# Gate and up products of a feature tile in two PSUM chains, with T4 negated: an fp32 hybrid encoder on one Trainium2 core

## The chip, the cores and the metric

The kernel runs on one core of a Trainium2 chip. The metric is device time in microseconds (us) of one execution. The engines are TensorE (PE: matmuls, and PEld: its weight loads), VectorE (DVE), ScalarE (ACT), GpSimd (POOL) and SyncE (SP, which issues most DMAs). Each engine takes its instructions in the order in which the program has them; engines wait for one another by semaphores. Results of matmuls land in PSUM, in banks of 128 x 512 fp32 values; VectorE and ScalarE read them from there.

## The reference

Two batches (512 prompt and 256 sample tokens, 768 in all, width 1024) go through two layers of an encoder. A layer is a mixer (differential attention beside a bidirectional mLSTM) and a gated feed-forward part with a convolution over positions. The change touches only this part:

```python
def _conv_ffn(x, w_gu, conv_w, conv_b, w_down):
    gu = x @ w_gu
    gate, up = gu[..., :D_FF], gu[..., D_FF:]          # D_FF = 2816
    gp = jnp.pad(gate, ((0, 0), (half, half), (0, 0)))
    conv = conv_b.astype(gate.dtype) + sum(gp[:, j:j + S] * conv_w[j] for j in range(CONV_WIDTH))
    hmid = jax.nn.gelu(conv, approximate=False) * up
    return hmid.astype(x.dtype) @ w_down
```

All is fp32.

## The kernel before

A matrix product in fp32 is made of three matmuls on parts: each operand is split into a high and a low part (hi and lo), and hi hi, hi lo, lo hi are added up in PSUM. The split of a weight block of 128 x 512 is a "conversion": ScalarE writes the high part wh (line 171), VectorE subtracts it for the low part wl (line 172). Weights come by DMA on SP's queue into a ring of six pieces (raw), and their parts go into twelve slots; a slot is filled again when the product that used it has ended.

The feed-forward part takes the 2816 features as 22 tiles of 128 per layer. For a tile it needs gate and up, each 128 features x 768 tokens. It computes both as one 2 x 2 block product by the scheme of Strassen and Winograd: seven products in place of eight. The tokens' blocks are A11, A12, A22 and the sums S1 to S4, all made once per layer. The weights' blocks are g0, g1, u0, u1 (halves of the rows of gate and up) and the combinations T1 to T4, which POOL (T1, T3) and VectorE (T2, T4) make at line 149 for each tile. A product is 12 matmuls of 128x384 at line 915 (four steps over k, three passes) into one bank. `bank()` hands out banks in turn by the string FTAGS of six tags; there are three banks of tag d, two of s, one of t, u and L each.

A tile's function `ff_tile` writes its seven products p1, p2, p4, p6, p7, p5, p3 one after the other, and the sums of Winograd's scheme between them: ScalarE copies p1 (line 927, m1), VectorE does the rest in seven operations with one operand in PSUM (lines 931 to 947). Then follow the convolution over positions (ScalarE line 948, VectorE lines 950 and 951, each in two pieces), the gelu (line 952), the product with up (line 953) and its split into high and low parts (lines 957, 958). g_lo, g_hi, up_lo, up_hi in this document are the halves of gate and up by tokens.

Tiles come in groups of 3 (the last of 4). After the first tile of the next group `down(gi)` multiplies the group's results by w_down (matmuls of 128x512, line 975) and VectorE adds the products to `acc` (line 982; for the first group line 980). The banks for this are of tags t and u in turn, and the three of d in the last group, after which the second LayerNorm follows tile by tile.

A scheduler sets the order on each engine: it takes instructions as they are ready, by a priority that is their place in the program, less an offset (for conversions of weights 100 places earlier). So the products of one tile and the next can be interleaved on TensorE.

## Time and profile before

| | us |
|---|---|
| median of 3 runs | 1888.2 (1887.25 to 1888.33) |
| the profiled execution: span from first to last instruction | 1882.1 |
| TensorE busy | 1838.9 (98%) |
| VectorE busy | 1342.5 (71%) |
| ScalarE busy | 771.7 (41%) |
| GpSimd busy | 238.8 (13%) |

The span is the time from the first to the last instruction that the profiler recorded; what lies around it belongs to the device time too. Matmuls overlap in the array, so that the listed duration of one (some 340 ns) is longer than the distance from one to the next, and that distance is what counts. In rows of a timeline the columns are start in us, duration in us, engine, line, operation, output and inputs, and in brackets the idle time of the engine before it with what ended it; "x2" means two instructions in a row.

### The profile page before, as it was taken

Reading aid. Unit: us, or ns where it says so; the run is one execution under the profiler, and the core shown is the slowest. Engines: PE = TensorE matmul, PEld = TensorE weight load, DVE = VectorE, ACT = ScalarE, POOL = GpSimd, SP = SyncE. Lnnn points to the kernel's source line nnn. Section 1 sums busy time; section 2 is a strip of 40 time slices with the busy share of each in tenths; the row PEclk is TensorE's granted clock in tenths of the full one; section 3 lists DMA queues with packets and bytes.
Section 4 is the critical chain, followed back from the end, with each engine's and each line's share of the span. In section 5 each row is a group of like instructions: output and inputs, shape, how many; then the busy total and the mean of one; then the engine's idle time right before and its main releaser. Section 6 shows DMA issues by size and latency. Waiting matters only on the chain. (4 is left out here: it accounts for less than half of the span.)

```text
span 1882.1 us, 26221 instructions
## 1 busy us (share of the span) xinstructions
PE 1838.9 (98%) x9692; PEld 1592.7 (85%) x9692; DVE 1342.5 (71%) x2576; ACT 771.7 (41%) x1624; POOL 238.8 (13%) x256
## 2 busy tenths in 40 slices
PE   8899999999999999999998999999999999999998
PEld 8777777779899899899897777777898998998996
DVE  5445776489886786787954457765898877877878
ACT  4344565334443343343332445654253432433330
POOL 1000101042110111110110011010411111111102
PEclk9999999999999999999999999999999999999999
DMA  6212110311222121122233021104022221221221
GB/s 196 85 49 68 46 45 23 135 40 62 85 81 66 59 82 62 64 77 87 100 107 90 18 68 51 40 23 150 25 68 96 68 79 62 71 76 57 79 62 67
DMA packets 83279, 134.94 MB, mean 72 GB/s; under 512 B 7984, under 2 KB 27056, under 8 KB 83152
## 3 DMA queue, kind: packets, MB, share of 16 engines
q1 hardware_dynamic: 82432, 132.90, 22.0%
q8 instruction: 76, 1.25, 0.3%
q14 instruction: 51, 0.42, 0.1%
q10 hardware_dynamic: 720, 0.37, 0.1%
HBM read 126.86 MB, written 6.39 MB: 71 GB/s over the span
## 5 line engine op out<-in xcount | busy, mean ns | idle before, releaser
L915 PE MATMUL p<-actA,wh 128*128 128x384 f32 x1408 | 363.4, 338 | 3.2 <-DVE g L940 3.2
L171 ACT ACTIVATE wh<-raw 128x512 fp32r<-128x512 f32 (+1 forms) x348 | 215.7, 629 | 299.8 <-PE p L915 109.7
L172 DVE TENSOR_TENSOR wl<-raw,wh 128x512 fp32r<-128x512 f32 (+1 forms) x348 | 242.7, 707 | 95.9 <-ACT wh L171 95.4
L915 PE MATMUL p<-actB,wh 128*128 128x384 f32 x1056 | 270.1, 337 | 0.0
L915 PEld LDWEIGHTS p<-actA,wh 128*128 128x128 f32 x1408 | 254.7, 188 | 5.8 <-DVE g L940 3.8
L915 PE MATMUL p<-actA,wl 128*128 128x384 f32 x704 | 237.3, 337 | 0.0
L149 POOL TENSOR_TENSOR T<-raw,raw 128x512 f32<-128x512 f32 x88 | 120.7, 1374 | 836.5 <-DVE wl L172 483.6
L975 PE MATMUL dn<-wh,actB 128*128 128x512 f32 x576 | 208.7, 396 | 1.1 <-DVE acc L982 1.1
L171 ACT ACTIVATE wh<-T 128x512 fp32r<-128x512 f32 x176 | 108.3, 628 | 220.2 <-DVE acc L982 105.0
L915 PEld LDWEIGHTS p<-actB,wh 128*128 128x128 f32 x1056 | 191.2, 188 | 0.0
L975 PE MATMUL dn<-wh,ring 128*128 128x512 f32 x480 | 179.2, 397 | 1.8 <-DVE acc L982 1.8
L915 PE MATMUL p<-actB,wl 128*128 128x384 f32 x528 | 177.2, 336 | 0.0
L982 DVE TENSOR_TENSOR acc<-acc,dn 128x512 f32<-128x512 f32 x144 | 98.1, 681 | 72.0 <-PE dn L975 71.8
L172 DVE TENSOR_TENSOR wl<-T,wh 128x512 fp32r<-128x512 f32 x176 | 129.6, 748 | 22.1 <-ACT wh L171 21.9
L975 PEld LDWEIGHTS dn<-wh,actB 128*128 128x128 f32 x576 | 108.0, 188 | 28.7 <-DVE acc L982 2.8
L915 PEld LDWEIGHTS p<-actA,wl 128*128 128x128 f32 x704 | 132.2, 188 | 0.1
L871 PE MATMUL wo<-wh,actB 128*128 128x512 f32 x384 | 122.7, 396 | 0.0
L975 PE MATMUL dn<-wl,actB 128*128 128x512 f32 x288 | 113.2, 393 | 0.0
L975 PEld LDWEIGHTS dn<-wh,ring 128*128 128x128 f32 x480 | 90.0, 188 | 24.8 <-DVE acc L982 4.4
L915 PEld LDWEIGHTS p<-actB,wl 128*128 128x128 f32 x528 | 99.1, 188 | 0.0
L356 PE MATMUL aqkA<-actA,wh 128*128 128x512 f32 x256 | 97.7, 407 | 0.0
L975 PE MATMUL dn<-wl,ring 128*128 128x512 f32 x240 | 94.6, 394 | 0.0
(263 smaller groups left out, 3442.8 us busy)
## 6 DMA issues: line engine op xcount, KB each, us to landing
raw<-in_w_g_dram SPq DMA_DIRECT2D x88, 256.0 KB, 2.7
raw<-in_w_u_dram SPq DMA_DIRECT2D x88, 256.0 KB, 2.7
raw<-in_w_down_dram SPq DMA_DIRECT2D x88, 256.0 KB, 2.9
raw<-in_w_out_dram SPq DMA_DIRECT2D x32, 256.0 KB, 2.6
pt<-scr_m SPq DMA_DIRECT2D x12, 512.0 KB, 5.9
raw<-in_w_c_dram SPq DMA_DIRECT2D x16, 264.0 KB, 3.9
raw<-in_w_av_dram SPq DMA_DIRECT2D x16, 256.0 KB, 4.8
raw<-in_w_aq_dram SPq DMA_DIRECT2D x16, 256.0 KB, 3.5
```

The source lines that it names most:

```text
L149: src["engine"].tensor_tensor(out=src["tile"], in0=a, in1=b, op=ALU.subtract)
L171: self.nc.scalar.activation(h, v, AF.Identity)
L172: self.nc.vector.tensor_tensor(out=l, in0=v, in1=h.bitcast(F32), op=ALU.subtract)
L356: PE.matmul(psA, w, actA[:, k, b, SB:T], start=n == 0, stop=n == 23)
L871: PE.matmul(p, actB[:, k, a, t * 128:(t + 1) * 128], units[k][1 + b], start=n + i == 0, stop=n == 7 and i == 2)
L915: PE.matmul(ps, blk[1 + a][:, k * 128:(k + 1) * 128], x[:, k, b, :], start=k + i == 0, stop=k == 3 and i == 2)
L975: PE.matmul(p, x, (wh_, wl_)[b], start=k + i == 0, stop=k == nf - 1 and i == 2)
L982: V.tensor_tensor(out=z, in0=z, in1=p, op=ALU.add)
```

## The change

- Three turns of `bank()` per tile in place of seven. A11, S2, S3 and A22 go into one bank px without its being cleared between, S1 and S4 into a second, pz; A12 has p2. Between the products of px its partial sum is copied to SBUF by ScalarE: m1 after A11, u2 after S2, u3 after S3, and g_hi at the end. pz is read after S1 (up_hi = pz + u3) and after S4 (up_lo = pz + u2).
- The order of a tile's products is A11, A12, S2, S1, S3, S4, A22.
- T4 has the other sign (g1 - T2), so that A22's product can be added into px. The order of the weight blocks follows the products.
- The sums on VectorE are three for a tile (g_lo, up_hi, up_lo), the copies on ScalarE four.

The rest of the diff takes out comments.

```diff
-                t4 = {"a": t2, "b": g1, "tag": "T4", "engine": V}
-                for src in (t4, t2, t3, t1, u1) if i in early else (g0, g1, t4, t2, t3, t1, u1):
+                t4 = {"a": g1, "b": t2, "tag": "T4", "engine": V}
+                for src in (t2, t1, t3, u1, t4) if i in early else (g0, g1, t2, t1, t3, u1, t4):
                     W.block(src, 512)
...
-        def product(ps, x):
+        def product(ps, x, first=True, last=True):
             blk = W.take()
             for k in range(4):
                 for i, (a, b) in enumerate(PASSES):
-                    PE.matmul(ps, blk[1 + a][:, k * 128:(k + 1) * 128], x[:, k, b, :], start=k + i == 0, stop=k == 3 and i == 2)
+                    PE.matmul(ps, blk[1 + a][:, k * 128:(k + 1) * 128], x[:, k, b, :], start=first and k + i == 0,
+                              stop=last and k == 3 and i == 2, skip_group_check=True)
             W.done(blk)
...
-            p1 = bank(f"p1_{f}")
-            product(p1, A11)
-            S.copy(m1, p1)
+            px = bank(f"px_{f}")
+            product(px, A11, last=False)
+            S.copy(m1, px)
             p2 = bank(f"p2_{f}")
             product(p2, A12)
             yield
             V.tensor_tensor(out=g[:, lo_], in0=p2, in1=m1, op=ALU.add)
-            p4 = bank(f"p4_{f}")
-            product(p4, A22)
-            p6 = bank(f"p6_{f}")
-            product(p6, S2)
-            V.tensor_tensor(out=u2, in0=p6, in1=m1, op=ALU.add)
-            p7 = bank(f"p7_{f}")
-            product(p7, S3)
-            V.tensor_tensor(out=u3, in0=p7, in1=u2, op=ALU.add)
-            V.scalar_tensor_tensor(out=g[:, hi_], in0=p4, scalar=-1.0, in1=u3, op0=ALU.mult, op1=ALU.add)
-            p5 = bank(f"p5_{f}")
-            product(p5, S1)
-            V.tensor_tensor(out=u4, in0=p5, in1=u2, op=ALU.add)
-            V.tensor_tensor(out=up[:, hi_], in0=p5, in1=u3, op=ALU.add)
-            p3 = bank(f"p3_{f}")
-            product(p3, S4)
-            V.tensor_tensor(out=up[:, lo_], in0=p3, in1=u4, op=ALU.add)
+            product(px, S2, first=False, last=False)
+            S.copy(u2, px)
+            pz = bank(f"pz_{f}")
+            product(pz, S1, last=False)
+            product(px, S3, first=False, last=False)
+            S.copy(u3, px)
+            V.tensor_tensor(out=up[:, hi_], in0=pz, in1=u3, op=ALU.add)
+            product(pz, S4, first=False)
+            product(px, A22, first=False)
+            S.copy(g[:, hi_], px)
+            V.tensor_tensor(out=up[:, lo_], in0=pz, in1=u2, op=ALU.add)
```

Three places in the first layer's tile 8, an ordinary one, show what this does to the order. In the names the number behind the first underscore is the tile; p6, p7 and p4 are the products with S2, S3 and A22; numbers behind wh and wl count the weight blocks, and the last number is the buffer's. "waits" lists the semaphores (an engine, or a DMA queue of the hardware) that the instruction waits for.

TensorE before, from the end of A22's product through S2's to the start of S3's:

```order
L915 MATMUL p4_8_5758<-actA_70,wl147_5532 128x384
L915 MATMUL p6_8_5777<-actB_2870,wh148_5537 128x384 x2
L915 MATMUL p6_8_5777<-actB_2870,wl148_5538 128x384
L915 MATMUL p6_8_5777<-actB_2870,wh148_5537 128x384 x2
L915 MATMUL p6_8_5777<-actB_2870,wl148_5538 128x384
L915 MATMUL p6_8_5777<-actB_2870,wh148_5537 128x384 x2
L915 MATMUL p6_8_5777<-actB_2870,wl148_5538 128x384
L915 MATMUL p6_8_5777<-actB_2870,wh148_5537 128x384 x2
L915 MATMUL p6_8_5777<-actB_2870,wl148_5538 128x384
L915 MATMUL p7_8_5797<-actB_2870,wh149_5543 128x384 [waits DVE_49]
```

TensorE after, from S3's product to the start of S4's:

```order
L915 MATMUL px_8_5667<-actB_2870,wh149_5499 128x384 x2
L915 MATMUL px_8_5667<-actB_2870,wl149_5500 128x384
L915 MATMUL px_9_5822<-actA_70,wh152_5566 128x384 x2
L915 MATMUL px_9_5822<-actA_70,wl152_5567 128x384
L915 MATMUL px_9_5822<-actA_70,wh152_5566 128x384 x2
L915 MATMUL px_9_5822<-actA_70,wl152_5567 128x384
L915 MATMUL px_8_5667<-actA_70,wh151_5547 128x384 [waits Activation_49]
L915 MATMUL px_8_5667<-actA_70,wh151_5547 128x384
L915 MATMUL px_8_5667<-actA_70,wl151_5548 128x384
L915 MATMUL px_8_5667<-actA_70,wh151_5547 128x384 x2
L915 MATMUL pz_8_5728<-actA_70,wh150_5525 128x384 [waits DVE_49]
L915 MATMUL pz_8_5728<-actA_70,wh150_5525 128x384
```

Before, a product runs through its twelve matmuls, and waits only for the reader that a bank had some products earlier. After, S3's product is followed by six matmuls of the next tile (px_9), then five of A22 into px_8, which wait for ScalarE, then S4 into pz_8, which waits for VectorE.

ScalarE before, from the split of tile 7 to the conversion that follows tile 8's convolution:

```order
L957 ACTIVATE ring_4085<-up7_5551 128x384 [waits DVE_49]
L957 ACTIVATE ring_4085<-up7_5551 128x384
L171 ACTIVATE wh158_5749<-raw127_5535 128x512 [waits DMAHW1_49,PE_49]
L171 ACTIVATE wh159_5771<-raw129_5592 128x512 [waits DMAHW3_49,PE_49]
L171 ACTIVATE wh160_5790<-raw130_5594 128x512 [waits DMAHW4_49,PE_49]
L171 ACTIVATE wh161_5810<-raw131_5655 128x512 [waits DMAHW5_49,PE_49]
L948 ACTIVATE c8_5713<-g8_5711,convw_220 128x768 [waits DVE_49,Activation_49]
L171 ACTIVATE wh162_5831<-raw132_5697 128x512 [waits DMAHW6_49,PE_49]
```

ScalarE after, from the copy u2 to the copy u3 and the conversion behind it:

```order
L935 COPY u2_8_5665<-px_8_5667 128x384 [waits PE_49]
L954 ACTIVATE ring_4075<-up7_5507 128x384 [waits DVE_49]
L954 ACTIVATE ring_4075<-up7_5507 128x384
L171 ACTIVATE wh160_5741<-raw130_5551 128x512 [waits DMAHW4_49,PE_49]
L171 ACTIVATE wh161_5759<-raw131_5608 128x512 [waits DMAHW5_49,PE_49]
L939 COPY u3_8_5666<-px_8_5667 128x384 [waits PE_49]
L171 ACTIVATE wh162_5779<-raw132_5646 128x512 [waits DMAHW6_49,PE_49]
```

The copy u3_8 stands right behind the conversion of wh161; S3 of this tile is block 149, and 161 is the block that takes its slot, twelve blocks on.

VectorE before, the sums of tile 8:

```order
L172 TENSOR_TENSOR wl159_5772<-raw129_5592,wh159_5771 128x512 [waits DMAHW3_49,PE_49,Activation_49]
L936 TENSOR_TENSOR u2_8_5715<-p6_8_5777,m1_8_5714 128x384 [waits PE_49]
L172 TENSOR_TENSOR wl160_5791<-raw130_5594,wh160_5790 128x512 [waits DMAHW4_49,Activation_49]
L939 TENSOR_TENSOR u3_8_5716<-p7_8_5797,u2_8_5715 128x384 [waits DVE_49,PE_49]
L172 TENSOR_TENSOR wl161_5811<-raw131_5655,wh161_5810 128x512 [waits DMAHW5_49,Activation_49]
L940 SCALAR_TENSOR_TENSOR g8_5711<-p4_8_5758,u3_8_5716 128x384 [waits DVE_49]
L943 TENSOR_TENSOR u4_8_5717<-p5_8_5818,u2_8_5715 128x384 [waits PE_49]
L944 TENSOR_TENSOR up8_5712<-p5_8_5818,u3_8_5716 128x384
```

VectorE after, the same stretch of tile 8:

```order
L955 TENSOR_TENSOR ring_4075<-up7_5507,ring_4075 128x384 [waits Activation_49] x2
L172 TENSOR_TENSOR wl160_5742<-raw130_5551,wh160_5741 128x512 [waits DMAHW4_49,PE_49,Activation_49]
L172 TENSOR_TENSOR wl161_5760<-raw131_5608,wh161_5759 128x512 [waits DMAHW5_49,PE_49,Activation_49]
L940 TENSOR_TENSOR up8_5662<-pz_8_5728,u3_8_5666 128x384 [waits DVE_49,Activation_49]
L149 TENSOR_TENSOR T2_167_5892<-raw137_5763,T1_167_5890 128x512 [waits DMAHW3_49,Pool_49]
L944 TENSOR_TENSOR up8_5662<-pz_8_5728,u2_8_5665 128x384 [waits PE_49]
```

Five sums with low parts of weights between them have become two; up_hi (line 940) stands behind two low parts, and the combination T2 for a later tile behind it.

## Rows read from the trace of the kernel before

**Rows 1.** The page: span, busy time by engine, granted clock in 40 slices.

```profile
span 1882.1 us, 26221 instructions
PE 1838.9 (98%) x9692; PEld 1592.7 (85%) x9692; DVE 1342.5 (71%) x2576; ACT 771.7 (41%) x1624; POOL 238.8 (13%) x256
PEclk9999999999999999999999999999999999999999
```

**Rows 2.** The chain of waits: start, length, engine, what, instructions; a whole group.

```profile
1447.88 44.08 PE p L915 x252
```

**Rows 3.** Waits of TensorE: total us, times, longest.

```profile
PE p L915 <- DVE g L940: 3.2, 2, 1.6
PE dn L975 <- DVE acc L982: 2.9, 10, 0.5
```

**Rows 4.** Groups of instructions by line: busy us, mean ns, idle before.

```profile
L939 DVE TENSOR_TENSOR u<-p,u 128x384 f32<-128x384 f32 x44 | 24.5, 556 | 29.1 <-PE p L915 29.1
L944 DVE TENSOR_TENSOR up<-p,u 128x384 f32<-128x384 f32 x44 | 24.0, 546 | 0.0
L927 ACT COPY m<-p 128x384 f32<-128x384 f32 x44 | 20.4, 463 | 0.2
L948 ACT ACTIVATE c<-g,convw 128x768 f32<-128x768 f32 x44 | 45.4, 1031 | 69.7 <-DVE g L940 69.7
L951 DVE SCALAR_TENSOR_TENSOR c<-g,convw,c 128x255 f32<-128x255 f32 x88 | 54.6, 659 | 0.0
L149 DVE TENSOR_TENSOR T<-raw,T 128x512 f32<-128x512 f32 x44 | 32.1, 730 | 18.3 <-POOL T L149 18.3
```

**Rows 5.** Timeline of a feature tile in the second layer, TensorE, ScalarE, VectorE.

```profile
1798.35 0.63 ACT L171 ACTIVATE wh<-T 128x512 fp32r<-128x512 f32 x1 [1.28 <-PE p L915]
1798.89 0.46 ACT L927 COPY m<-p 128x384 f32<-128x384 f32 x1
1799.86 0.51 PE L915 MATMUL p<-actA,wh 128*128 128x384 f32 x2
1800.41 0.63 ACT L171 ACTIVATE wh<-raw 128x512 fp32r<-128x512 f32 x1 [1.06 <-PE p L915]
1806.49 0.34 PE L915 MATMUL p<-actB,wl 128*128 128x384 f32 x1
1806.86 0.56 DVE L939 TENSOR_TENSOR u<-p,u 128x384 f32<-128x384 f32 x1 [0.93 <-PE p L915]
```

**Rows 6.** Timeline at the first layer's feed-forward start, VectorE, GpSimd, TensorE.

```profile
442.57 4.10 DVE L172 TENSOR_TENSOR wl<-raw,wh 128x512 fp32r<-128x512 f32 x3
442.13 3.39 POOL L149 TENSOR_TENSOR T<-raw,raw 128x512 f32<-128x512 f32 x2 [6.19 <-DVE wl L172]
446.16 0.34 PE L915 MATMUL p<-actB,wh 128*128 128x384 f32 x1
447.52 0.54 DVE L940 SCALAR_TENSOR_TENSOR g<-p,u 128x384 f32<-128x384 f32 x1
448.12 0.62 PE L915 MATMUL p<-actA,wh 128*128 128x384 f32 x2 [1.62 <-DVE g L940]
```

**Rows 7.** Timeline at the second layer's end, TensorE, ScalarE, VectorE.

```profile
1840.26 0.39 PE L975 MATMUL dn<-wh,ring 128*128 128x512 f32 x1
1842.16 0.85 ACT L952 ACTIVATE c<-c 128x768 f32<-128x768 f32 x1 [3.66 <-DVE c L951]
1844.59 1.03 DVE L958 TENSOR_TENSOR actB<-up,actB 128x384 fp32r<-128x384 f32 x2 [0.59 <-ACT actB L957]
1845.74 1.39 DVE L982 TENSOR_TENSOR acc<-acc,dn 128x512 f32<-128x512 f32 x2
1874.13 0.69 DVE L982 TENSOR_TENSOR acc<-acc,dn 128x512 f32<-128x512 f32 x1 [0.98 <-PE dn L975]
```

More of the change, by code (lines that the diff above doesn't have):

```diff
@@ L922, in ff_tile @@
             c = ft.tile([128, T], F32, tag="c", name=f"c{f}")
-            m1, u2, u3, u4 = (ft.tile([128, HALF], F32, tag=t, name=f"{t}_{f}") for t in ("m1", "u2", "u3", "u4"))
+            m1, u2, u3 = (ft.tile([128, HALF], F32, tag=t, name=f"{t}_{f}") for t in ("m1", "u2", "u3"))
             lo_, hi_ = slice(0, HALF), slice(HALF, T)
-            p1 = bank(f"p1_{f}")
-            product(p1, A11)
-            S.copy(m1, p1)
+            px = bank(f"px_{f}")
+            product(px, A11, last=False)
+            S.copy(m1, px)
             p2 = bank(f"p2_{f}")
```

## The prediction

> **What bounds the kernel now.** I read the page first: TensorE is busy 1838.9 us of the 1882.1 us span, VectorE 1342.5, ScalarE 771.7, and the row of granted clock shows a nine in each of its 40 slices [rows 1]. A busy share proves little by itself, so I went to the chain of waits: in the feed-forward part it is one unbroken run on TensorE, for example 252 matmuls of line 915 in 44.08 us, which is 0.175 us for one matmul, 2.1 us for a product of 12 and 14.7 us for a feature tile of seven [rows 2]. Then the waits of TensorE: line 915 waits 3.2 us in all for VectorE (two waits of 1.6), and line 975 waits 2.9 us for the accumulations, in ten pieces [rows 3]. The reader is to see two things. TensorE sets the pace of this stage, so work taken from VectorE gives nothing unless TensorE had waited for it; and what it had waited for is small. A matmul that waited also lets its successor begin late, so the loss is a little more than the wait: at the two starts of the feed-forward part 448.12 - 446.16 - 0.175 = 1.78 us [rows 6] and about the same in the second layer, 3.5 in all; at the group ends the 2.9 us and 0.1 to 0.25 for each of ten, 4 to 5.4. So about 9 us, 0.5% of the time, is all that lighter engines could return. Counts of matmuls don't change: 44 tiles of 84 in both kernels.
>
> The whole question is then whether the new order of reads makes TensorE wait. Before, each product took the next of six banks in turn, and no matmul waited for the read of the product just ahead of it. Now px is written, read, written again: TensorE must not go on with px until ScalarE has copied it.
>
> **The change part by part.**
>
> *What is removed.* Four of seven VectorE operations with a PSUM operand go for each tile (546 to 556 ns each [rows 4]): 44 x 4 x 0.55 = 97 us of VectorE. Three more copies of 463 ns [rows 4] come to ScalarE: 44 x 3 x 0.46 = 61 us. Both are off the path, and worth nothing by themselves.
>
> *Latencies.* From the start of a product's last matmul (1806.49) to the operation that reads its bank (1806.86) are 0.37 us; the same 0.37 lie between the eleventh matmul of a product, the second of the pair at 1799.86, thus at 1800.04, and the conversion that refills its weight slot (1800.41) [rows 5]. After a conversion the next instruction on ScalarE starts 0.54 later (1798.35 to 1798.89) [rows 5]. From the end of a VectorE operation (447.52 + 0.54) to the released matmul at 448.12 are 0.06 us, and that matmul's successor starts 0.28 instead of 0.175 after it, since its weights could not be loaded ahead [rows 6].
>
> *m1 before S2, u2 before S3.* Between the write and the next use of px lie 12 matmuls of another bank, 2.1 us. The copy needs 0.37 + 0.46 + 0.06 = 0.89 us, and with one conversion in front 1.43. Hidden, at nothing; the cover is the twelve matmuls of p2 and of S1.
>
> *u3 before A22.* Here the scheduler puts only six matmuls of the next tile between, 1.05 us (five down matmuls at the tiles ahead of a down step). Let t be the start of S3's last matmul. On ScalarE the instruction just ahead of the u3 copy is, in 40 of 44 tiles, the conversion that waits for S3's own weight slot: it starts at t - 0.175 + 0.37 = t + 0.20, the copy at t + 0.74, ends at t + 1.20, and A22's weights can be loaded at about t + 1.25. Undisturbed they would be loaded at t + 1.05. That is 0.20 us late, of which about 0.07 lies in the weight load that runs ahead: some 0.14 us per tile. The lower bound is nothing (the copy alone, with no conversion in front, ends at t + 0.83), the upper 0.35, where the conversion starts 0.2 later because its source is late. 42 tiles (the tail stands below) x 0.14 = **+5.9 us**, between 0 and 15. Queued behind a late copy on ScalarE are the next conversions, which have a weight ring of twelve slots in front of them; on VectorE the up_hi addition waits for the same copy.
>
> *up_hi before S4.* pz is read by VectorE (line 940) before S4 may add to it. Cover: after the copy's release five matmuls of A22, 0.875 us; the addition needs 0.05 + 0.55 + 0.06. Since VectorE has a weight's low part (0.6) just ahead, the addition ends at about t + 2.05, and S4's load is due then. At nothing, in ordinary tiles.
>
> *New weight order.* T2 now comes third and T4 last. In the first tiles of each group VectorE holds T2 and T4 (730 ns one [rows 4]) ahead of the convolution, whose result the next tile does not need at once. In twelve tiles I see the u2 copy come to its limit; 0 to 0.5 us each, I take 0.17: **+2 us**, between 0 and 6.
>
> *Group ends.* The loss at line 975 comes from accumulations on a full VectorE [rows 3]. With 97 us less on it most of that should go. But g_hi is now the last product, so the convolution (four operations near 0.66 [rows 4]) falls among these accumulations. **-4 us**, between -5.4 and -1.
>
> *The two starts.* Before, VectorE works off seven low parts, the last three in 4.10 us while POOL computes T1 and T3 beside it, and TensorE stands from the start of the matmul at 446.16 to 448.12 [rows 6]. In the new queue the same seven low parts, now with T2 and T4, stand ahead of up_hi, while u2 and u3 have left it: 1.2 us more for two combinations, 1.0 less for two additions. **+1 us** for both layers, between -3.5 (all of the wait gone) and +5.
>
> *The tails.* In the last tile of a layer g_hi was read during the product p7, so the gelu started 1.9 us after the first down matmul (1840.26, 1842.16), and the first accumulation 3.58 after that [rows 7]. Now the chain starts only behind the last product: copy at 0.20, 0.46 long, convolution by ScalarE 1.03 [rows 4], four VectorE operations 2.3, so the gelu at 4.1, 2.2 later than before. Down matmuls that need nothing of this tile cover 3 banks x 9 x 0.23 = 6.3 us, against low parts ready at about 7.0: TensorE waits 0.8. The accumulations after it fill VectorE, and the slack ahead of the last of them is 0.98 us [rows 7], so the end moves by 0.8 to 2.8; I take 1.5 per layer: **+3 us**, between 1.6 and 5.6.
>
> *Against the rule on banks.* What the rows show: with six banks in turn line 915 waited only at the two starts [rows 3]. The Trainium skill, Perfetto Trace Analysis, section Optimizing Tensor Performance / Matmuls, says that independent groups of matmuls should rotate through PSUM banks so that the evacuation of one lies beside the matmuls of the next. It speaks against a bank that is taken up four times in one tile: with nothing of another bank between, each of three re-entries per tile would cost the 0.89 us of a copy with its latencies, 3 x 44 x 0.89 = +117 us. The order leaves 12, 12 and 6 matmuls of other banks between, so that by the rows only the last is short, and the sum stays as it is worked out here.
>
> **Sum.** 5.9 + 2 - 4 + 1 + 3 = +7.9 us, span 1890.0. The median of the runs stands 6.1 us above the span (1888.2 against 1882.1), which I leave as it is: **1896 us**, 0.4% slower. A measurement of this kernel can tell about 0.2%, 3.8 us, from no change.
>
> **Rivals.**
> 1. *The copies hide, only the relief is left.* If the scheduler's cover suffices (u3 starts before the conversion or is released earlier), the first term is 0, the second 0, group ends -5.4, starts 0, tails +1.6 or so: -4, about 1884; with the starts' 3.5 gone too, 1881. For it: 1.05 us of cover against 0.89 for a bare copy. Against it: the fixed place of the conversion in front, on an engine that works in order.
> 2. *ScalarE's queue decides.* If the conversion ahead of u3 waits for its DMA piece or for a combination of POOL, the copy waits with it and TensorE stands. One such conversion more in front of the copy is 0.54 us [rows 5]: with 0.6 per tile, 42 x 0.6 = +25, less the rest at about 0, some 1913. It decides once a conversion's source lands later than its slot comes free. For it: ScalarE and VectorE take every conversion in order. Against it: in the steady stretch the conversions waited for TensorE (the matmul's slot) and not for their source [rows 5].
> 3. *The clock.* The row of granted clock shows nines throughout, the level of 2.4 GHz, also past the waits of 1.6 us [rows 1, 3]. If some 42 new short waits let it fall to 1.2 GHz for a tenth of the feed-forward products (3696 x 0.175 = 647 us), that would be +65 us, about 1955. The Trainium skill, TensorE: Matmul & The Clock Gate, section A second HAM failure mode: psum-queue depth-cycling, reports such an oscillation where TensorE pauses shortly between matmul groups; no row here shows one.
>
> **How the numbers follow.** Forecast (the sum, 1890 to 1904): 0.50, of which 0.07 lies within 0.2%. Rival 1: 0.33, of which 0.20 is faster by over 0.2% and 0.13 within. Rival 2: 0.14. Rival 3: 0.03. So faster 0.20, same 0.20, slower 0.60. Terms at their ends give -10 to +34 us; all at one end is unlikely. The range goes from 1882 to 1911: it leaves out the better part of rival 1's gain below (0.07), half of rival 2 and rival 3 above (0.10).
>
> **What would show it.** Right: a wait of line 915 for the copy of line 939 in about 40 tiles, 0.1 to 0.2 us each; group ends with less wait for the accumulations than 2.9 us; a first accumulation in the last stretch some 2 us later after the products' end. Waits for m1 or u2 would show a wrong reading of their cover; no waits at all for u3, rival 1; waits of half a microsecond and conversions that wait for DMA or POOL, rival 2; a slice of granted clock under nine, rival 3. The prediction would be wrong above all if u3's copy gets a place ahead of the conversion in time, or if ScalarE is late by more than this one conversion.

## The result, and the profile after

The changed kernel takes 1913.6 us (median of four runs, 1912.4 to 1914.8) against 1887.8 for the kernel before: 1.0138 times as long, 95% interval 1.0123 to 1.0152, or 25.7 us more. The prediction said slower, and 1896 us with a range of 1882 to 1911. The sign was right, the size three times too small.

The page of the changed kernel, as in [rows 1]:

```profile
span 1910.6 us, 26212 instructions
PE 1853.3 (97%) x9692; PEld 1590.4 (83%) x9692; DVE 1269.8 (66%) x2400; ACT 826.1 (43%) x1756; POOL 240.9 (13%) x256
PEclk9999999999999999999999999999999999999999
```

VectorE has lost 73 us of work (97 for the sums; its low parts of weights now take some 30 more, 781 ns in place of 707 for those straight from DMA, and other operations a little less) and ScalarE gained 54. A slice of the page is 48 us long, so its row of nines would not show a short stretch at a lower clock. The two feed-forward parts by themselves (stretch, its length, busy time and instructions of PE, PEld, DVE, ACT and POOL, granted clock, share of DMA, GB/s):

```profile
423.67:956.00 532.33, 523.48 (x2710) 475.71 (x2709) 384.59 (x595) 227.30 (x395) 68.66 (x56) 1.00 0.23 73
1372.40:1901.50 529.10, 519.54 (x2679) 472.20 (x2677) 378.07 (x584) 217.26 (x378) 69.27 (x56) 1.00 0.21 68
```

The clock is 1.00, the level of 2.4 GHz, in both, as in the kernel before; what brings the mean to 0.993 lies outside them. So the time is not made of slower matmuls. The waits of TensorE in the feed-forward part, as in [rows 3] (engine, line waited for, total us, times, longest):

```profile
PE px L915 <- ACT u L935: 8.7, 12, 1.4
PE pz L915 <- DVE up L940: 3.3, 2, 1.7
PE dn L972 <- ACT actB L954: 2.3, 2, 1.6
PE px L915 <- ACT u L939: 1.9, 2, 0.9
```

All are new. The accumulations of [rows 3] are no longer in the list, though the down steps still lose some 4.4 us by them in smaller pieces. The largest row isn't the copy u3 (line 939) that the prediction watched, but u2 (line 935): 12 waits, one in the first tile of each group but the layer's first, up to 1.4 us.

To see the sum of it I took, for all matmuls of the feed-forward part, the distance from one start to the next, less 0.175 us for a product's matmul and 0.2325 for a down matmul, and added up what is over 0.05 us ("late matmuls"). Beside it stands the length of the two feed-forward parts, from the first product to the last down matmul, and of the rest ahead of them (mixers, projections, norms), all in us:

| kernel | time | against before, 95% | feed-forward parts | rest | late matmuls |
|---|---|---|---|---|---|
| before (the trace shown) | 1887.8 | | 1037.0 | 829.6 | 14.5 |
| before_again | 1888.8 | one run | 1037.3 | 834.2 | 14.7 |
| after | 1913.6 | 1.0123 to 1.0152 | 1061.4 | 832.7 | 36.9 |
| t4_pool | 1903.5 | 1.0069 to 1.0099 | 1052.4 | 834.4 | 28.5 |
| a22_own | 1904.5 | 1.0077 to 1.0114 | 1054.7 | 830.8 | 31.3 |
| seven_banks | 1900.4 | 1.0051 to 1.0081 | 1050.2 | 831.9 | 26.9 |
| u2_only | 1891.6 | 1.0012 to 1.0030 | 1040.4 | 833.3 | 17.6 |
| u2_t4p | 1895.0 | 1.0026 to 1.0048 | 1044.5 | 831.1 | 21.5 |
| late_s4 | 1913.7 | 1.0110 to 1.0144 | 1052.5 | 849.8 | 29.2 |
| late_t4p | 1921.8 | 1.0159 to 1.0192 | 1058.8 | 847.8 | 35.6 |
| late40 | 1897.2 | 1.0036 to 1.0066 | 1047.9 | 831.1 | 24.7 |
| start7 | 1910.0 | 1.0103 to 1.0135 | 1059.7 | 830.7 | 35.1 |
| mixed | 1890.2 | 1.0007 to 1.0024 | 1041.5 | 832.1 | 18.4 |
| mixed_sw | 1895.0 | 1.0027 to 1.0054 | 1043.2 | 833.3 | 18.9 |

The kernel before stood at 1886.8 to 1888.3 us beside these runs. In every kernel the feed-forward parts are longer than before by what the late matmuls have grown, to 2.1 us or less. Of the changed kernel's 24.4 us, 22.4 are late matmuls. So the question is which matmuls are late, and behind what.

In eight of the variants some late matmuls waited for nothing: the clock was low. The first down matmuls of seven_banks, behind a wait of 3.75 us:

```profile
498.40:501.90 3.50, 3.50 (x9) 2.72 (x10) 2.92 (x5) 1.11 (x3) 0.00 (x0) 0.51 0.17 41
501.90:505.00 3.10, 3.10 (x15) 2.53 (x14) 1.96 (x3) 0.00 (x0) 0.00 (x0) 1.00 0.14 55
```

The granted clock is at its level of 1.2 GHz, then at 2.4 again; down matmuls follow one another at 0.43 us in the first stretch, and product matmuls at 0.32 in such stretches of other variants. Of the late matmuls this makes at least 1.4 us in t4_pool, 1.3 in a22_own, 2.5 in seven_banks, 1.4 in u2_t4p, 5.9 in late_s4, 5.1 in late_t4p, 1.4 in late40 and 2.8 in mixed. Each such stretch began during, or at most 1.1 us after, a wait of TensorE of 1.8 to 4.2 us (two waits in a row in t4_pool, 2.4 and 0.9, and in mixed's first layer, 1.3 and 0.5). The length of a wait doesn't decide it alone: S4 comes 2.15 us late in the first tile of both layers of a22_own, and only in the second did the clock fall. Each kernel was traced once.

**The largest item: u2.** The first tile of the second group in the first layer, TensorE's wait and what led to it, by engine (start, duration, engine, line; in brackets the idle time before and what ended it):

```profile
477.48 1.80 POOL L149 TENSOR_TENSOR T<-raw,raw 128x512 f32<-128x512 f32 x1 [0.24 <-DMA raw<-in_w_u_dram]
479.31 0.88 SPq L140 DMA_DIRECT2D raw<-in_w_g_dram  x2
482.39 0.69 DVE L149 TENSOR_TENSOR T<-raw,T 128x512 f32<-128x512 f32 x1 [1.96 <-DMA raw<-in_w_g_dram]
483.00 1.14 DVE L947 SCALAR_TENSOR_TENSOR c<-g,convw,c 128x255 f32<-128x255 f32 x2
484.06 1.14 DVE L948 SCALAR_TENSOR_TENSOR c<-g,convw,c 128x255 f32<-128x255 f32 x2
485.29 0.84 ACT L949 ACTIVATE c<-c 128x768 f32<-128x768 f32 x1 [3.06 <-DVE c L948]
486.04 0.61 ACT L171 ACTIVATE wh<-raw 128x512 fp32r<-128x512 f32 x1
486.56 0.46 ACT L935 COPY u<-px 128x384 f32<-128x384 f32 x1
487.07 0.61 PE L915 MATMUL px<-actB,wh 128*128 128x384 f32 x2 [1.13 <-ACT u L935]
```

Read it from the bottom: S3's matmul waits 1.13 us for the copy u2 (486.56). The copy itself was ready to go long before, but on ScalarE it stands behind a conversion (486.04) and the gelu of the tile before (485.29). The gelu waits for the convolution on VectorE (483.00, 484.06). The convolution stands behind a combination T4 for a later tile (482.39), for which VectorE sits idle for 1.96 us until a weight piece has come by DMA. That DMA was issued at 479.31, as soon as POOL's combination (477.48, 1.80 us long) had ended and let a piece of the ring go. In all twelve places T4 waits for its piece, and the piece is issued right at the end of a POOL combination. Two engines that work in order carry a load that POOL held up into a copy that has nothing to do with it.

**The item that was predicted: u3.** A steady tile:

```profile
529.35 0.34 PE L915 MATMUL px<-actB,wl 128*128 128x384 f32 x1
529.54 0.63 ACT L171 ACTIVATE wh<-T 128x512 fp32r<-128x512 f32 x1 [1.45 <-PE px L915]
530.08 0.46 ACT L939 COPY u<-px 128x384 f32<-128x384 f32 x1
530.39 0.34 PE L915 MATMUL px<-actA,wl 128*128 128x384 f32 x1
530.60 0.62 PE L915 MATMUL px<-actA,wh 128*128 128x384 f32 x2
```

S3's last matmul starts at 529.35; the conversion that its slot lets go starts 0.19 later, the copy 0.73 later, and it ends 1.19 later. A22's first matmul stands at 530.60 where 530.565 would be undisturbed, and its successor starts 0.28 after it. That is 0.14 us for the tile.

**The starts.** The first and second tile of the first layer:

```profile
447.79 1.41 DVE L149 TENSOR_TENSOR T<-raw,T 128x512 f32<-128x512 f32 x2
449.11 0.55 DVE L940 TENSOR_TENSOR up<-pz,u 128x384 f32<-128x384 f32 x1
449.71 0.62 PE L915 MATMUL pz<-actA,wh 128*128 128x384 f32 x2 [1.66 <-DVE up L940]
458.87 1.28 ACT L949 ACT_TABLE_LOAD   x1 [1.02 <-DVE c L948]
460.16 0.84 ACT L949 ACTIVATE c<-c 128x768 f32<-128x768 f32 x1
460.91 0.46 ACT L939 COPY u<-px 128x384 f32<-128x384 f32 x1
461.43 0.62 PE L915 MATMUL px<-actA,wh 128*128 128x384 f32 x2 [0.93 <-ACT u L939]
```

In the first tile S4 waits 1.66 us for up_hi, behind the combinations, much as g_hi did in [rows 6]. In the second tile A22 waits another 0.93 for u3, which stands behind a gelu, and that behind the load of the gelu's table of 1.28 us, which itself began when VectorE's convolution (line 948) was done. Before, ScalarE held this table load too (1.28 us at 451.79), but no matmul waited for anything behind it. S1, now needed ahead of S3 though its operand is made after, costs another 0.5 us in each layer.

**The tail.** The end of the second layer, as in [rows 7]:

```profile
1867.90 0.39 PE L972 MATMUL dn<-wh,ring 128*128 128x512 f32 x1
1868.10 0.48 ACT L943 COPY g<-px 128x384 f32<-128x384 f32 x1 [4.58 <-PE px L915]
1871.97 0.85 ACT L949 ACTIVATE c<-c 128x768 f32<-128x768 f32 x1 [2.33 <-DVE c L948]
1874.42 0.50 PE L972 MATMUL dn<-wh,actB 128*128 128x512 f32 x1 [0.77 <-ACT actB L954]
1875.65 1.28 DVE L979 TENSOR_TENSOR acc<-acc,dn 128x512 f32<-128x512 f32 x2 [0.23 <-PE dn L972]
```

The gelu starts 4.07 us after the first down matmul here (1.90 in [rows 7]), the first accumulation 7.75 (5.48 before): 2.3 later. TensorE's matmul at 1874.42 waited 0.77.

### The profile page after: what moved, and what is told of

Same layout as the page of the kernel before. It is cut to its first block, busy times and chain, and to the rows that moved or that the text cites. A ratio compares the mean times of both kernels' runs of the same rounds, so it can differ in the third digit from the quotient of the medians.

```text
span 1910.6 us, 26212 instructions
## 1 busy us (share of the span) xinstructions
PE 1853.3 (97%) x9692; PEld 1590.4 (83%) x9692; DVE 1269.8 (66%) x2400; ACT 826.1 (43%) x1756; POOL 240.9 (13%) x256
## 5 line engine op out<-in xcount | busy, mean ns | idle before, releaser
L172 DVE TENSOR_TENSOR wl<-raw,wh 128x512 fp32r<-128x512 f32 (+1 forms) x348 | 268.0, 781 | 125.4 <-ACT wh L171 124.4
L149 POOL TENSOR_TENSOR T<-raw,raw 128x512 f32<-128x512 f32 x88 | 128.5, 1464 | 846.5 <-DVE wl L172 485.8
L915 PE MATMUL px<-actA,wh 128*128 128x384 f32 x704 | 188.1, 344 | 2.0 <-ACT u L939 1.9
L915 PE MATMUL px<-actB,wh 128*128 128x384 f32 x704 | 181.6, 339 | 8.7 <-ACT u L935 8.7
L915 PEld LDWEIGHTS px<-actB,wh 128*128 128x128 f32 x704 | 126.4, 188 | 13.1 <-ACT u L935 13.1
L915 PEld LDWEIGHTS px<-actA,wh 128*128 128x128 f32 x704 | 125.0, 188 | 13.0 <-ACT u L939 11.4
L915 PE MATMUL px<-actA,wl 128*128 128x384 f32 x352 | 118.7, 337 | 0.0
L915 PE MATMUL px<-actB,wl 128*128 128x384 f32 x352 | 118.3, 336 | 0.0
L149 DVE TENSOR_TENSOR T<-raw,T 128x512 f32<-128x512 f32 x88 | 63.1, 717 | 60.9 <-DMA raw<-in_w_u_dram 25.4
L915 PE MATMUL pz<-actA,wh 128*128 128x384 f32 x352 | 91.5, 341 | 3.3 <-DVE up L940 3.3
```

The lines of the kernel that those rows point to most:

```text
L149: src["engine"].tensor_tensor(out=src["tile"], in0=a, in1=b, op=ALU.subtract)
L172: self.nc.vector.tensor_tensor(out=l, in0=v, in1=h.bitcast(F32), op=ALU.subtract)
L915: PE.matmul(ps, blk[1 + a][:, k * 128:(k + 1) * 128], x[:, k, b, :], start=first and k + i == 0, stop=last and k == 3 and i == 2, skip_gro ...
```

## The experiments

**before_again: the kernel before, once more.**

> The kernel before, once more, with a profile. The changed kernel's trace is longer by 28.5 us of span, of which some 24 lie in the feed-forward parts and 3.5 in the mixers, whose code is the same. Theory: the mixers' part is a difference between executions, and the trace of before was a short one: the span now comes out at 1885 to 1887 us, with the feed-forward stretches (first to last matmul of line 915) at 482.8 and 483.3 us as in the first trace. Rival: the mixers are slowed by the change (banks, the order of the first weights): the span is 1882 us again, with the mixers as in the first trace.

```profile
span 1886.9 us, 26221 instructions
```

The feed-forward parts are equal to 0.3 us, and the rest is 4.6 us longer than in the trace shown ahead, longer even than in the changed kernel. So the mixers' 3.2 us in the comparison of the two traces belong to the execution, and nearly the whole of the change's 25.7 us lies in the feed-forward parts and the end (24.4 and 0.7). The clock makes a part of that difference: in the rest it stood at 1.2 GHz for 13.7 us in the trace shown, for 20.5 in before_again and in after. The 6.8 us between are worth 3.4 at most, of 4.6. In the changed kernel's runs the time stands 1.75 us above the span; the 6.1 us of the prediction came from a trace that was some 4 us shorter than the runs beside it.

**t4_pool: T4 off VectorE.**

```diff
-                t4 = {"a": g1, "b": t2, "tag": "T4", "engine": V}
+                t4 = {"a": g1, "b": t2, "tag": "T4", "engine": G}
```

> The changed kernel with T4 made on POOL in place of VectorE, so that a T4 that waits for its DMA no longer stands ahead of the convolution on VectorE. Theory: in the first tile of a group the matmuls of S3 wait for the copy u2, which stands behind the gelu on ScalarE, which waits for the convolution, which stands behind T4: with T4 gone from VectorE the 8.7 us of waits on line 935 fall under 2, and the time from 1913.5 to 1901 to 1905 us. Rival: the length of ScalarE's queue by itself (gelu and conversions ahead of the copy) makes these waits: they stay over 6 us, the time at 1911 to 1916.

1903.5 us, 10.1 less than the changed kernel. The same place as above, now with T4 on POOL:

```profile
482.16 1.15 DVE L947 SCALAR_TENSOR_TENSOR c<-g,convw,c 128x255 f32<-128x255 f32 x2 [0.37 <-ACT c L945]
484.46 0.85 ACT L949 ACTIVATE c<-c 128x768 f32<-128x768 f32 x1 [0.63 <-DVE c L948]
485.82 0.46 ACT L935 COPY u<-px 128x384 f32<-128x384 f32 x1
```

The order on ScalarE is the same (gelu, conversion, copy), but the convolution waits only for its own input. TensorE's list of waits has no row of line 935 left: the chain from the DMA to u2 is shown, and ScalarE's queue by itself doesn't make it. What comes instead stands at the starts:

```profile
PE px L915 <- ACT u L939: 4.6, 2, 2.3
```

The late matmuls within 40 us of the start rise from 12.3 to 14.6 us, of which 1.4 are a stretch at 1.2 GHz in the second layer.

**a22_own: A22 in a bank of its own, third, T4 in its old place.**

```diff
+            p4 = bank(f"p4_{f}")
+            product(p4, A22)
             product(px, S2, first=False, last=False)
...
-            product(px, S3, first=False, last=False)
+            product(px, S3, first=False)
             S.copy(u3, px)
             V.tensor_tensor(out=up[:, hi_], in0=pz, in1=u3, op=ALU.add)
+            V.tensor_tensor(out=g[:, hi_], in0=p4, in1=u3, op=ALU.add)
             product(pz, S4, first=False)
-            product(px, A22, first=False)
-            S.copy(g[:, hi_], px)
```

> A22 has a bank of its own again and comes third, T4 has its old sign and place; A11, S2, S3 stay in the chain px and S1, S4 in pz. So the late T4, the short cover of u3 and the exposed gate at a layer's end are undone, the copies between products are kept, each with 11 or 12 matmuls to hide under. Theory: a copy with that cover costs nothing, and VectorE is lighter: 1884 to 1890 us, no waits on the copies over 1 us in sum. Rival: taking up a bank again costs by itself some 0.1 us each time, whatever the cover (2 to 3 times in 44 tiles): 1897 to 1901 us, with a late matmul at each of these places.

(T4's sign stays the new one in this kernel, so that g_hi is a plain sum; its place is the old one.)

1904.5 us: my theory was wrong by some 15 us, and the rival, a cost for each re-entry, isn't it either. Outside the starts S2 and S3 take up px again in every tile without a late matmul; all the loss in the tiles is at one place, S4 behind up_hi:

```profile
PE pz L915 <- DVE up L942: 7.0, 10, 2.0
```

Eleven matmuls, 1.9 us, lie between S3 and S4 there, and yet 68 matmuls of S4 are late there, 10.5 us in all: up_hi must wait for the copy u3 on ScalarE, then stands on VectorE behind a low part, and TensorE waits for both. S4 stands where the scheduler took up_hi to be ready, as I read it: the longer cover is no slack, only a longer way to cover. The down steps lose 10.7 us here, 6.4 before.

**seven_banks: the order alone.**

```diff
-            product(px, S2, first=False, last=False)
-            S.copy(u2, px)
-            pz = bank(f"pz_{f}")
-            product(pz, S1, last=False)
...
+            p6 = bank(f"p6_{f}")
+            product(p6, S2)
+            V.tensor_tensor(out=u2, in0=p6, in1=m1, op=ALU.add)
+            p5 = bank(f"p5_{f}")
+            product(p5, S1)
+            V.tensor_tensor(out=u4, in0=p5, in1=u2, op=ALU.add)
...
+            p4 = bank(f"p4_{f}")
+            product(p4, A22)
+            V.tensor_tensor(out=g[:, hi_], in0=p4, in1=u3, op=ALU.add)
```

> The changed kernel's order of products and of weights and its T4, but seven products in banks of their own, with the sums on VectorE as before. Theory: the waits come from the chains, and the order costs only the exposed gate at the ends and the starts: 1888 to 1894 us. Rival: the order with the late T4 costs by itself, since VectorE, now with all seven sums, stands behind T4 and holds banks: 1900 us or more, with waits of line 915 for VectorE in the first tiles of the groups.

1900.4 us, in the rival's range but not at its place. In the tiles no matmul is late (0.1 us in sum), and the starts lose 8.2 us as before (8.0). 18.6 us are lost at the down steps (6.4 before), most at the first group's end:

```profile
494.44 2.14 DVE L952 SCALAR_TENSOR_TENSOR c<-g,convw,c 128x255 f32<-128x255 f32 x2
496.50 1.13 DVE L953 SCALAR_TENSOR_TENSOR c<-g,convw,c 128x255 f32<-128x255 f32 x2
497.56 1.27 DVE L982 SCALAR_TENSOR_TENSOR acc<-acc,dn 128x512 f32<-128x512 f32 x2
498.29 0.64 PE L977 MATMUL dn<-wh,actB 128*128 128x512 f32 x1 [3.75 <-DVE acc L982]
```

With g_hi from the last product the convolution (lines 952 and 953) of the tile just ahead falls beside the first down matmuls, and the accumulations that free their banks (line 982) stand behind it: 3.9 us late here, and as much in the second layer. At both waits the clock fell to 1.2 GHz, which is at least 2.5 of the 18.6 us. So the order costs by itself, 13.3 us in the feed-forward parts, the slow clock behind its waits included, with VectorE as full as before; the chains, which relieve VectorE, take this loss away and bring their own.

**late_s4 and late_t4p: a longer cover.**

```diff
-            product(pz, S4, first=False)
-            product(px, A22, first=False)
+            with prio(PR_L):
+                product(pz, S4, first=False)
+                product(px, A22, first=False)
```

with PR_L = -40 (in late_t4p with T4 on POOL too).

> The changed kernel with a lower priority for the products S4 and A22: twelve matmuls of the next tile stand between S3 and them in place of six (eight down matmuls in place of five in a group's first tile). Theory: the 0.1 us by which a matmul comes late at A22 (39 places, 3.8 us in all) and at S4 (13 places, 1.4 us) is a cover too short by that much, and goes: 1907 to 1910 us, with the 10.6 us of the first tiles' waits for u2 unchanged or up to 3 us more, since the gate is finished later. Rival: a matmul that waits for a semaphore costs 0.1 us however early the event: these places stay, 1912 to 1916 us.

> Both at once: the longer cover, and T4 on POOL. Theory: the two costs are separate and add: 1903.5 for T4 on POOL alone, less 5 for the cover: 1897 to 1900 us. Rival: the later gate takes back what the cover gives, or one wait takes the place of the other: 1902 us or more.

1913.7 and 1921.8 us, and useless as times: the name PR_L was in use for the mLSTM, whose order changed with it, and the rest ahead of the feed-forward parts grew by 20.2 and 18.2 us over the trace of before (the mean granted clock of the two traces is 0.986 and 0.987). Only the feed-forward parts can be read: 8.9 us shorter than after's in late_s4, 2.6 in late_t4p, though they hold 5.9 and 5.1 us of slow clock. So the rival of late_t4p holds there: the cover and the moved T4 don't add up.

**late40: the longer cover alone.** The same edit with the number -40 in place of the name.

> late_s4 again with its priority written as a number: the name used there for it already set the order of the mLSTM's work, so that the mixers were put in another order too. Here only S4 and A22 of a tile have the lower priority. Theory, from the feed-forward stretches of late_s4, which were 8.4 us shorter in both layers together than those of the changed kernel: 1904 to 1907 us, with no late matmul at A22, no wait for u2, and a tail wait of 4 us per layer in place of 1.7. Rival: the mixers' 16 us of late_s4 come from the feed-forward part in another way than by their order: 1911 us or more.

1897.2 us: 16.4 less than the changed kernel, where I expected 1904 to 1907; the feed-forward parts gave 13.5 of it, 4.6 more than in late_s4, whose feed-forward parts hold some 4.5 us more of slow clock. A22 is late nowhere, and the waits for u2 are gone as well, for another reason than in t4_pool. The same place again, ScalarE:

```profile
483.65 0.46 ACT L935 COPY u<-px 128x384 f32<-128x384 f32 x1
485.23 0.85 ACT L950 ACTIVATE c<-c 128x768 f32<-128x768 f32 x1 [1.11 <-DVE c L949]
```

T4 still waits for its DMA there, and the gelu is no earlier, but the copy u2 now stands ahead of the gelu. That separates the two causes: the late T4 and the copy's place behind the gelu cost only together. What is left (10.9 us in the feed-forward parts):

```profile
PE dn L973 <- ACT actB L955: 7.5, 2, 4.0
PE pz L915 <- DVE up L940: 4.7, 5, 1.7
```

a tail three times as long, since A22 of the last tile comes still later, with 1.4 us of slow clock behind the wait of 4.0, and S4 late by 0.09 us in 30 places and by more in four.

**u2_only and u2_t4p: one link of the chain in the kernel before.**

```diff
-            p6 = bank(f"p6_{f}")
-            product(p6, S2)
-            V.tensor_tensor(out=u2, in0=p6, in1=m1, op=ALU.add)
+            product(px, S2, first=False)
+            S.copy(u2, px)
```

(p1 is px here, left open for S2; u2_t4p has T4 on POOL as well.)

> The kernel before with one link of the chain alone: A11 and S2 share a bank, u2 is a copy by ScalarE, one VectorE sum less per tile; order of products and weights, T4, and all else as before. The re-entry of S2 has 24 matmuls of cover, and nothing in TensorE's order waits for u2. Theory: taking up a bank again costs nothing where the copy is long done; VectorE's relief of 24 us gives 0 to 2 us at the group ends: 1885 to 1889 us. Rival: a re-entry costs 0.1 us by itself: 44 x 0.1 = +4.4, 1890 to 1893 us.

> The same with T4 (old sign, old place) on POOL, another 30 us off VectorE. Theory, if VectorE's load makes the waits at the group ends (some 5 us) and at the starts (3.5 us): 1882 to 1886 us, faster than the kernel before. Rival: POOL takes 1.4 us for a combination in place of 0.7 and slows VectorE's low parts beside it, as at the start of the feed-forward part with T4 on POOL in the changed kernel: 1887 to 1892 us.

1891.6 and 1895.0 us. In neither is S2's matmul late once, behind 24 matmuls of cover: taking up a bank again costs nothing by itself, which the rival of u2_only had at 4.4 us. But my theory of a small gain is wrong too: the down steps lose 10.3 and 13.3 us (6.4 before; 1.4 of the 13.3 are slow clock). In u2_only, first layer's first group:

```profile
501.26 0.69 DVE L149 TENSOR_TENSOR T<-raw,T 128x512 f32<-128x512 f32 x1 [1.85 <-POOL T L149]
501.99 0.69 DVE L149 TENSOR_TENSOR T<-T,raw 128x512 f32<-128x512 f32 x1
502.60 0.68 DVE L980 SCALAR_TENSOR_TENSOR acc<-acc,dn 128x512 f32<-128x512 f32 x1
503.34 0.50 PE L975 MATMUL dn<-wh,actB 128*128 128x512 f32 x1 [1.23 <-DVE acc L980]
```

VectorE has been idle for 1.85 us when POOL's combination comes, does two combinations, and only then the accumulation that a matmul has waited 1.23 us for. In VectorE's order these two stand ahead of the fifth accumulation of the step, in the kernel before ahead of the eighth: with less work on VectorE, later tiles' combinations are placed earlier. So less load on VectorE doesn't shorten the waits at the group ends by itself; here what stands ahead of an accumulation decides.

**start7, mixed and mixed_sw: the border tiles.** In start7 the first two tiles of each layer have the seven banks of seven_banks; mixed is late40 with the first two and the last tile in the kernel before's form; mixed_sw is that with A22 ahead of S4.

The choice of the form in mixed (the diff leaves out the two forms, seven banks and the two chains):

```diff
+            if f < FF_EARLY or f == 21:
...
+            else:
...
```

> The changed kernel, but the first two tiles of each layer have seven banks and VectorE's sums, in the same order of products and weights. Theory: the extra loss at the two starts (12.3 us of late matmuls against 8.0 before; 8.2 with seven banks in all tiles) comes from the chains there, since u3 and up_hi wait behind the low parts and the gelu's table: 1908 to 1911 us, with no wait of 0.9 us for u3 in the second tile. Rival: the order of weights in the first tiles makes it: 1912.5 us or more.

1910.0 us, in the theory's range, but for half of its reason: the late matmuls within 40 us of the start fall from 12.3 to 8.1, as they should, and 2.6 us come back behind them: the first two tiles with chains wait for u3 by 0.75 and 0.93 us in the first layer, which in the changed kernel they did not. The feed-forward parts gain 1.7.

> late40, but the first two and the last tile of each layer are computed as in the kernel before (seven banks, its order of products and weights, only T4's sign new). Theory: the costs are separate and local. late40 has 24.7 us of late matmuls in the two feed-forward parts; without its two tail waits (some 8 us) and the extra loss at the starts (4 us) some 12.5 remain, against 14.5 in the kernel before: 1884 to 1888 us, level with the kernel before or up to 0.2% faster. Rival: the border tiles only hand the waits on to their neighbours, the first and last tiles in the chain form: 1890 to 1896 us.

1890.2 us, above the theory's range and at the rival's edge. The tail's waits are gone; the starts keep the wait for g_hi that the kernel before has, the first down step waits for a tile's high parts, and S4 is late by 2.5 us in all behind up_hi:

```profile
PE p L915 <- DVE g L943: 3.6, 2, 1.8
PE dn L999 <- ACT ring L981: 2.1, 2, 1.2
```

Another 2.8 us are slow clock, one stretch in each layer behind the waits of these two rows. Less these, the trace's feed-forward parts are within 2 us of the kernel before. This is the best version with chains, and by its interval (1.0007 to 1.0024) still slower than the kernel before.

> The same with A22 ahead of S4 in the chain tiles (and T4 ahead of u1): up_hi then has A22's matmuls to hide under, and the gate is finished earlier. A22 gets six matmuls of cover again. Theory of the short cover: the 30 places at S4 (2.7 us) lose their lateness, A22's 0.1 us comes back in the steady tiles (28 x 0.1): within 2 us of mixed. Rival, if the earlier gate is what matters: 2 us or more faster than mixed; if the gate's copy in front of the gelu on ScalarE brings the waits for u2 back: 1895 us or more.

1895.0 us, the last rival: A22 late again in 40 places (3.9 us) and by 1.5 us in two more, the waits for u2 back (1.6 us in two), S4 late nowhere. The down steps lose 0.6 us in all, the least of any kernel here, and it doesn't help.

## Why the prediction was right or wrong

- *TensorE sets the pace, and the question is which matmul waits.* Right: the table above closes on late matmuls alone.
- *u3 before A22, +5.9 us.* Right in mechanism and size: 0.14 us at the tile shown, as forecast to the hundredth (conversion at 0.19, copy at 0.73, end at 1.19 against 0.20, 0.74 and 1.20). 39 successors are late by 0.1, 3.8 us, and with the few hundredths of the first matmuls it is some 5. late40 takes them away by cover alone.
- *up_hi before S4, nothing.* Nearly: 13 places of 0.1, 1.4 us, at the tiles ahead of down steps. With another placement of S4 the same wait was ten (a22_own).
- *The new weight order, +2 us, between 0 and 6.* This is the step that failed, and with it *u2 before S3, hidden, at nothing*. The place was seen (T2 and T4 ahead of the convolution, the u2 copy at its limit in twelve tiles), but sized at 0.17 us a tile and bounded at 0.5. Measured in just these twelve tiles: 0.33 to 1.6 us, 10.6 in sum, and 1.3 more for the successors. The term counted only what T2 and T4 take (730 ns each), not what T4 waits for. In the trace above T4 waits 1.96 us for its piece, and the wait is handed on through convolution, gelu and copy; t4_pool and late40 each break this chain at another link, and the waits go. The prediction held this very case as its second rival (a copy behind work that waits for a DMA, 1913 us, chance 0.14), with the wrong copy: u3 and its conversion in place of u2 and the gelu. That its 1913 us is the measured time is luck: it was worked out for 42 tiles of 0.6 us, and the waits were in twelve, beside other losses.
- *Group ends, -4 us.* Half of it: with the tails' waits taken off, the down steps lose 4.4 us after against 6.4 before.
- *The two starts, +1 us, up to 5.* Mis-sized: 12.3 against 8.0, +4.3. The wait for up_hi is what was forecast (1.66 against 1.62 in [rows 6]); the wait for u3 in the second tile, behind the load of the gelu's table, and S1's operand were not seen.
- *The tails, +3 us.* Right in mechanism (gelu at 4.07 us, forecast 4.1; accumulation 2.3 later, forecast 2.2), and about right in sum, but unevenly shared: TensorE loses 1.8 us in the first layer's last down step, and in the second the down matmuls and the end together move by 0.8 to 0.9; 1.5 were taken for each.
- *Rival 1 (the copies hide).* Its claim that a lighter VectorE gives something back isn't borne out by u2_only: an operation less on it per tile (and a copy more on ScalarE), and the time 0.2% longer.
- *Rival 3 (the clock).* Right to set aside for the changed kernel: many more matmuls are late than before, and the clock stays at 2.4 GHz through both feed-forward parts. The evidence was weak, since the row of nines can't show a stretch of a few us, and eight variants had such stretches. The oscillation that the Trainium skill reports (TensorE: Matmul & The Clock Gate, section A second HAM failure mode: psum-queue depth-cycling) doesn't show in the changed kernel; in the variants the clock fell once to three times in the feed-forward parts, each time during or right behind a wait.
- *The rule on banks* (the Trainium skill, Perfetto Trace Analysis, section Optimizing Tensor Performance / Matmuls) does not by itself tell the price here, which goes by what stands in the queue of the copy: S2 taken up again behind 24 matmuls cost nothing in 44 tiles of u2_only, and S3 behind twelve of another bank cost up to 1.6 us where the copy's engine was held up.
- *The base.* That the time stands 6.1 us above the span was a property of one short trace; it didn't enter the difference.

What stays open: why mixed and late40 still lose 4.6 and 10.9 us in the feed-forward parts is listed by place, but no version was tried that takes away S4's lateness and the starts' at once. Whether T4's piece would come in time with a seventh piece in the ring, or with POOL's combinations done elsewhere, was not tried. Nor is it shown what makes the clock fall behind one wait and not behind another as long.

One correction to the words ahead of the prediction: the scheduler's offset of 100 places moves the conversions back, not forward (the offset of -40 in late40, of the same sign, moved S4 and A22 back); nothing in the sum used it.

## What to carry to other kernels

When a step is put between two uses of a buffer that the bounding engine needs, ask not only how long that step takes and how much work covers it, but what stands ahead of it on its own engine, what that waits for, and so on until a transfer or the bounding engine itself is reached; here a load that was issued late, behind a combination on POOL, went through VectorE's and ScalarE's queues into a copy. A cover that a scheduler chose is, as I read these runs, no slack: it puts the next use where it takes the step to be done, and a tenth of a microsecond per tile is lost. A table of late matmuls needs the granted clock beside it, since a long wait can be followed by slow matmuls that wait for nothing. Take work off an engine that isn't the bound only if a wait of the bounding engine ends on it, and look at its order before its load.

## What the runs showed of the hardware

- A bank that is read between two products and written on costs TensorE nothing where the copy is done in time: no late matmul at S2 in u2_only in 44 tiles.
- A matmul that waited for a few hundredths still makes its successor start 0.28 us after it in place of 0.175, in every kernel here: a wait costs 0.1 us more than it shows.
- The same program's mixers differ by 4.6 us between two executions (829.6 and 834.2), while its feed-forward parts differ by 0.3; the clock stood at 1.2 GHz in the rest for 13.7 and 20.5 us.
- During or right behind a wait of TensorE of 1.9 to 4.2 us the clock fell to 1.2 GHz in seven_banks, late40, u2_t4p and others, and down matmuls then came every 0.43 us in place of 0.2325; waits of 1.66 us in the changed kernel and of 2.5 in t4_pool's first layer left it at 2.4 GHz.
